# Eight small tiles of the second expert pass, fetched ahead of the weight ring

## The chip, the cores and the metric

The kernel runs on one core of a Trainium2 chip. The metric is device time in microseconds, the median of several runs; less is better.

## The reference

Two encoder layers over 512 frames of 1024 channels. Each has a token mixer (a convolution module in layer 0, a short gated convolution in layer 1) and then a mixture of experts; each part is wrapped in a conditioned residual and a layer norm. The change lies in the experts:

```python
g_idx = argmax(xf @ w_group + b_group)          # one of 4 groups for each frame
e_logits = (xf @ w_router + b_router)           # 32 experts, 8 in each group
top_p, top_e = top_k(softmax(e_logits of the group), 2)
hid = silu(xblk @ w_gate[e]) * (xblk @ w_up[e]) # w_gate, w_up: 1024 x 512
yb = hid @ w_down[e]                            # w_down: 512 x 1024
y = sum over a frame's two experts of weight * yb
```

All is float32, so an expert's three matrices are 6 MB and a layer's 32 experts 192 MB.

## The kernel before

**Passes.** The experts of a layer are handled in 14 passes (`PASSES`). A pass has 128 slots for frames, in four groups of 32 columns, shared by one to four experts: pass 0 has two experts with 64 slots each, pass 1 four experts with 32 each, pass 2 one expert with all 128. Experts are put in order of the number of frames that chose them, except that the first two places always hold experts 0 and 1, so that pass 0 can be fetched before anything is known of the routing. The other places' experts are known when the tile `ids` has been written (L1076); SyncE then loads the numbers of a pass into registers (`experts`, L154 to L160) when it comes to the first fetch of that pass.

**The ring.** All large weights go through the tag `ring` of six buffers of 2 MB (`R`, L107). `todo` lists the fetches in order; `pump` starts fetches while fewer than six units are out, `unit` takes the next one for use, and `done` gives one back and pumps. All these fetches are issued by SyncE, in the order of the list. A unit of an expert pass (`u_pass`, L169) holds two parts of 1 MB. Parts come in the order of `parts_of_pass` (L165): for the first half of the contraction the gate matrices of all the pass's experts, then their up matrices; the same for the second half; then the two halves of the down matrices. Pass 1 so has 24 parts, 0 to 23: 0 to 3 the four experts' first gate halves, and so on. A part's 8 KB for one partition are four rows of a matrix that lie one after another.

**A pass.** The loop over `t` from 0 to 15 (L1252) multiplies the slots with gate and up. Four steps of `t` share the parts of one kind; after the fourth, `release` gives back the ring units that are used up. In between, the loop issues other work for TensorE: `gather` of the next passes' inputs, `combine`, which adds the results of the pass before to the frames, and in pass 1 at `t == 1` the four scaling rows (`row`, L444) with which GpSimd scales the residual. Then come `hid`, its transposes and the down matmuls (L1327), and the results are scaled (L1339) and split into two float32r tiles each (`split`, L455) for `combine` in the next pass.

**Small tiles.** The tag `w2` has 21 buffers of 256 KB, for everything small that is passed between engines (`W`, L76): the logits' copies, one-hot matrices, rows, split results. An allocation takes a buffer that has come free; what first writes it waits for the last reader of what was there.

Before the last pass a branch (`beyond`, L1200) handles experts with more frames than slots; at this branch SyncE waits until its fetches have landed.

Of the kernel before, what the change touches and what calls it, by code (L numbers as in the profile page):

```python
# [37 lines left out]
RING = 6  # L38
NW2 = 21
LAST = 4  # L40
BIG = 1e30
FAR = 4096.0

PASSES = ((2, 2), (1, 1, 1, 1), (4,), (2, 2), (3, 1), (2, 2), (3, 1), (2, 1, 1), (2, 2), (3, 1), (2, 2), (3, 1),
          (2, 2), (1, 1, 1, 1))
# [17 lines left out]
def trunk_kernel(ctx: ExitStack, tc: tile.TileContext, x, c, ada_w, ada_b, a_w_in, a_b_in, a_w_dw, a_b_dw,  # L63
# [3 lines left out]
    nc = tc.nc  # L67
# [5 lines left out]
    def T(shape, dt, tag, bufs=1):  # L73
        return sb.tile(shape, dt, name=tag, tag=tag, bufs=bufs)

    def W(shape, dt=F32):  # L76
        return sb.tile(shape, dt, name="w2", tag="w2", bufs=NW2)
# [6 lines left out]
    def P(tag, shape=(128, 512)):  # L84
        return pp.tile(list(shape), F32, name="p" + tag, tag=tag, bufs=PB[tag])
# [5 lines left out]
    todo, have = deque(), deque()  # L91
# [8 lines left out]
    def unit():  # L100
        return have.popleft()

    def done(n=1):
        state["out"] -= n
        pump()

    def R(shape):  # L107
        return sb.tile(shape, F32, name="ring", tag="ring", bufs=RING)
# [10 lines left out]
    def u_ada1(i, v, kq):  # L119
        def f():  # L120
            t = R([128, 4, D])
            w = ada_w[i, kq * 512:(kq + 1) * 512, v * D:(v + 1) * D].rearrange("(k p) n -> p k n", p=128)
            for z in (slice(0, 3), slice(3, 4)) if kq else (slice(0, 4),):
                nc.sync.dma_start(t[:, z], w[:, z])
            return t
        return f
# [10 lines left out]
    def u_bin(nb):  # L137
        def f():
            t = R([128, 3, KD, 128])
            for z, part in enumerate((1, 2, 0)):  # L140
                nc.sync.dma_start(t[:, z], b_w_in[0, :, part * D + nb * 128:part * D + nb * 128 + 128]
                                  .rearrange("(k p) n -> p k n", p=128))
            return t
        return f

    def u_out(w, h):
        def f():
            t = R([128, 4, D])
            nc.sync.dma_start(t, w[h * 512:(h + 1) * 512, :].rearrange("(k p) n -> p k n", p=128))
            return t  # L150
        return f


    def experts(i, g):  # L154
        if g == 0:
            return [slice(0, 1), slice(1, 2)]
        if (i, g) not in ids:
            ids[i, g] = [bass.ds(nc.values_load(ids[i][:1, p:p + 1], engines=[ET.SP], min_val=0, max_val=NE - 1), 1)
                         for p in range(FIRST[g], FIRST[g] + len(PASSES[g]))]
        return ids[i, g]  # L160
# [4 lines left out]
    def parts_of_pass(n):  # L165
        return [(s, z, h) for h in range(2) for z in range(2) for s in range(n)] + \
               [(s, 2, u) for u in range(2) for s in range(n)]

    def u_pass(i, g, j):  # L169
        def f():  # L170
            t = R([128, 2, 2048])
            for y, (s, z, h) in enumerate(parts_of_pass(len(PASSES[g]))[2 * j:2 * j + 2]):
                w = (e_w_gate, e_w_up, e_w_down)[z][i, experts(i, g)[s]]
                nc.sync.dma_start(t[:, y], w.rearrange("o (p h k) n -> h p (o k n)", h=2, k=2 if z == 2 else 4)[h])  # L174
            return t
        return f


    def u_last(i, d):
        def f():  # L180
            n = len(PASSES[-1])
            t = R([128, n, 2, 512])
            for s, e in enumerate(experts(i, NP - 1)):
                nc.sync.dma_start(t[:, s], e_w_down[i, e].rearrange("o (p h k) n -> h p (o k) n", h=2, k=2)
                                  [1][:, :, d * 512:(d + 1) * 512])
            return t
        return f
# [9 lines left out]
    for i in range(DEPTH):  # L197
        if i == 1:
            todo += [u_bin(nb) for nb in range(2)]
            for nb in range(2, KD):  # L200
                todo += [u_ada1(1, 1 + nb // 2, nb % 2), u_bin(nb)]
        else:
            todo += [rest.popleft()]
        todo += [u_out((a_w_out, b_w_out)[i][0], h) for h in range(2)]
        todo += list(rest) if i == 0 else []
        todo += [u_ada1(1, v, kq) for v in ((1, 0), (5,))[i] for kq in range(2)]
        for g in range(NP):
            n = len(PASSES[g])
            if g < NP - 1:
                todo += [u_pass(i, g, j) for j in range(3 * n)]  # L210
            else:
                todo += [u_pass(i, g, j) for j in range(5 * n // 2)] + [u_last(i, d) for d in range(2)]

# [100 lines left out]
    for kind in set(PASSES):  # L314
        if len(kind) > 1:
            t = side[kind] = T([128, len(kind)], F32, "side%d" % (len(side),))
            V.memset(t, 0.0)
            o = 0
# [113 lines left out]
    def mod(i, v):  # L432
        return mods[i][:, v * 8:v * 8 + 8]
# [82 lines left out]
    class Out:  # L516
# [28 lines left out]
        def run(self, uT, pre, uh, ul, extra, turn, copies, logits, choose, fill, hook):  # L545
# [16 lines left out]

            last = range(KD - LAST, KD)

# [71 lines left out]
    for k in range(KD):  # L636
        p = P("a")
# [104 lines left out]
    w = None  # L742
    for nb in range(KD):
        if nb % 2 == 0:
            w = unit()
        s = slice((nb % 2) * 128, (nb % 2) * 128 + 128)
# [31 lines left out]
        if nb == 2:  # L778
            p = P("c")
# [49 lines left out]
    res = Out(grow, False)  # L829
# [27 lines left out]
    for i in range(DEPTH):  # L857
# [63 lines left out]
        def choose():  # L921
            for _ in zip_longest(first_max(e1, Fl(m1), El, Fl(kk)), first_max(go, gm, Lg, kg)):
                pass
            V.scalar_tensor_tensor(Ew, o1, -BIG, Ew, op0=OP.mult, op1=OP.add)
            for _ in first_max(e2, Fl(m2), El, Fl(kk)):
# [138 lines left out]
        t = by_expert(0)  # L1064
# [156 lines left out]
                PE.matmul(sums[q][d], ident, half(q, d), start=True, stop=False)  # L1221

        pend = None
        for g, kind in enumerate(PASSES):
            Q, j = g // 2, g % 2
            ns = len(kind)
# [2 lines left out]
            cols, o = [], 0  # L1229
# [8 lines left out]


            def piece(y):  # L1240
                while len(tiles) <= y // 2:
                    tiles.append(unit())
                return tiles[y // 2][:, y % 2].rearrange("p (k n) -> p k n", k=4)

            def release(y):
                nonlocal free
                while 2 * free + 2 <= y:
                    done()
                    free += 1

            pgu = [P("a"), P("a")]
            for t in range(2 * KD):  # L1252
                z, k = t // 4 % 2, t // 8 * 4 + t % 4
                if t % 4 == 0:
                    w = [piece(t // 4 * ns + s) for s in range(ns)]
                for s, a, b in cols:
                    PE.matmul(pgu[z][a:b, :], xe(Q, k, j)[:, a:b],  # L1257
                              w[s][:, t % 4, :], start=k == 0,
                              stop=k == KD - 1)
                if t % 4 == 3:  # L1260
                    release((t // 4 + 1) * ns)
                if g == 1:
                    if t == 1:
                        arow, brow = row(pcol("mg", i * 8, 8), ALPHA), row(pcol("mb", i * 8, 8), ALPHA)
                        for q in range(NQ):
                            scale_rows(q, arow, brow)
                    if t in (3, 6):
                        gather(1, 0 if t == 3 else 2)
                    for item in {7: (0,), 9: (1, 2), 11: (3, 4), 13: (5, 6)}.get(t, ()):
                        combine(pend, item)  # L1270
                elif t in (4, 8, 12):
                    combine(pend, t // 2 - 2)
                    combine(pend, t // 2 - 1)
                if g == 0:
                    if t in (1, 4):
                        gather(0, {1: 4, 4: 6}[t])
                    elif t == 6:
                        weigh()
                    elif t == 11:
                        counts()  # L1280
                        ohs.append(pair(1, Vd))
                if i == 0 and g == NP - 1 and t == 1:
                    nxt_aff = affine(pcol("fg", 0, 8), pcol("fb", 0, 8), mod(1, 1), mod(1, 0))
                if i == DEPTH - 1 and g == NP - 1 and t == 13:
                    arow, brow = row(pcol("fg", i * 8, 8)), row(pcol("fb", i * 8, 8))
                if t == 12 and g:
                    ws, C = slots_of(ohq, FIRST[g], kind)
# [15 lines left out]
            if g == 0:  # L1303
                GF = row(mod(i, 5))
                t = by_expert(1)
# [10 lines left out]
            for u in range(2):  # L1316
                last = g == NP - 1 and u == 1
                if last:
                    w = [unit(), unit()]
                    w = [[w[d][:, s] for d in range(2)] for s in range(ns)]  # L1320
                else:
                    w = [piece((4 + u) * ns + s) for s in range(ns)]
                    w = [[v.rearrange("p (f d) n -> p f d n", d=2)[:, :, d] for d in range(2)] for v in w]
                for x in range(4):
                    f, d = (x % 2, x // 2) if last else (x // 2, x % 2)
                    for s, a, b in cols:
                        PE.matmul(pd[d][a:b, :], hT[:, (2 * u + f) * 128 + a:(2 * u + f) * 128 + b], w[s][d][:, f, :],  # L1327
                                  start=u + f == 0, stop=u + f == 2)
# [11 lines left out]
            for d in range(2):  # L1340
                y = W([128, 512], F32R), W([128, 512], F32R)
# [20 lines left out]
        if i == DEPTH - 1:  # L1362
            for n in range(NQ + 1):
# [9 lines left out]
                for h in range(2):  # L1373
                    t = half(q, h)
# [41 lines left out]
        w = unit()  # L1416
# [48 lines left out]
        for nb in range(KD):  # L1465
# [31 lines left out]
            if nb == KD - 1:  # L1497
# [3 lines left out]
                res = Out(grow, True)  # L1501
# [8 lines left out]
            t = W([128, 512])  # L1510
# [35 lines left out]
```

## Time and profile before

| | us |
|---|---|
| median of 3 runs | 1492.92 (1492.81 to 1493.61) |
| profiled execution | 1491.18 |
| its span, first to last instruction | 1489.4 |

The profile is that of one execution. Times in its views are microseconds from the start of the span. PE is TensorE's matmul, PEld its weight load, DVE VectorE, ACT ScalarE, POOL GpSimd, SP SyncE; a "q" behind an engine's name is its sequencer, on which transfers are issued. A line number such as L1257 is a line of the kernel before. A float32 matmul of the program shows as two. A view of windows gives, for stretches of the span, each engine's busy time with the number of its instructions, the clock granted to TensorE, the share of the 16 DMA engines' time that was busy, and the rate.

### The profile page before, as it was taken

The page shows a single profiled execution, that of the slowest core. Times are in us where ns is not written, and L with a number is a line of the kernel's source. Part 1 is how long each engine was busy: PE and PEld are TensorE (multiplying, and loading weights), DVE is VectorE, ACT ScalarE, POOL GpSimd, SP SyncE. Part 2 cuts the span into 40 slices and gives each one's busy share as a digit, 9 for nine tenths or more (in the row PEclk, how much of TensorE's full clock was granted, in tenths as well). Part 3 has the DMA queues.
Part 4 walks back from the last instruction along what each step waited for, and adds up shares of the span by engine and source line. Part 5 has one row for each costly group of instructions (what it writes and reads, how often), then busy time and mean ns, then how long its engine had stood idle before and what let it go on. Part 6 is the DMA issues. An engine that isn't in the chain of part 4 may idle for free. (4 is left out here: it accounts for less than half of the span.)

```text
span 1489.4 us, 20667 instructions
## 1 busy us (share of the span) xinstructions
PE 1382.6 (93%) x8044; PEld 735.5 (49%) x8044; DVE 739.6 (50%) x1426; ACT 325.7 (22%) x547; POOL 263.9 (18%) x275
## 2 busy tenths in 40 slices
PE   4999898999999999997898989999999999999875
PEld 2444477544444444442286767874445444454322
DVE  2799988533343433332267876453334343343215
ACT  1465476210010011000061222422001000011001
POOL 1399942050000000000026051003100000000002
PEclk9999999999999999999999999989999999999988
DMA  8954344799999999999993745239999999999984
GB/s 295 396 213 177 117 154 174 280 420 421 422 419 420 418 421 420 421 421 387 376 279 127 232 173 179 108 147 413 421 421 417 410 416 422 421 421 420 420 356 150
DMA packets 112960, 488.68 MB, mean 328 GB/s; under 512 B 12483, under 2 KB 45771, under 8 KB 63691
## 3 DMA queue, kind: packets, MB, share of 16 engines
q1 hardware_dynamic: 108555, 486.84, 82.1%
q8 instruction: 67, 1.10, 0.3%
q0 software_dynamic: 128, 0.04, 0.2%
q10 hardware_dynamic: 4160, 0.30, 0.2%
q14 instruction: 50, 0.41, 0.1%
HBM read 485.02 MB, written 2.10 MB: 327 GB/s over the span
## 5 line engine op out<-in xcount | busy, mean ns | idle before, releaser
L1257 PE MATMUL pa<-ring,w 128*32 128x512 f32 (+2 forms) x2624 | 438.5, 604 | 26.6 <-DMA ring<-in_e_w_up_dram 15.1
L1131 DVE TENSOR_TENSOR X<-X,pb 128x512 f32<-128x512 f32 x208 | 133.9, 683 | 274.8 <-PE pb L1139 274.8
L1257 PEld LDWEIGHTS pa<-ring,w 128*32 128x32 f32 (+2 forms) x2624 | 120.8, 120 | 274.5 <-issue 227.9
L1327 PE MATMUL pa<-ring,w 128*32 128x512 f32 (+2 forms) x1312 | 209.0, 600 | 9.6 <-DMA ring<-in_e_w_down_dram 6.4
L1139 PE MATMUL pb<-w,w 128*128 128x512 f32 x416 | 130.1, 435 | 0.0
L1327 PEld LDWEIGHTS pa<-ring,w 128*32 128x32 f32 (+2 forms) x1312 | 60.9, 120 | 135.8 <-issue 113.5
L1339 DVE SCALAR_TENSOR_TENSOR w<-pa,ws,w 128x512 f32<-128x512 f32 x56 | 41.9, 750 | 164.9 <-PE pa L1327 162.3
L750 PE MATMUL pa<-RB,ring 128*128 128x512 f32 x256 | 116.5, 612 | 6.2 <-DMA ring<-in_a_w_in_dram 4.2
L1139 PEld LDWEIGHTS pb<-w,w 128*128 128x128 f32 x416 | 72.5, 193 | 97.5 <-issue 80.7
L695 POOL TENSOR_TENSOR w<-w,w 128x512 f32<-128x512 f32 x80 | 104.7, 1309 | 56.2 <-ACT w L693 50.6
L456 ACT ACTIVATE w<-w 128x512 fp32r<-128x512 f32 x58 | 36.6, 630 | 256.8 <-DVE w L1339 256.8
L457 POOL TENSOR_TENSOR RC<-w,RB 128x512 fp32r<-128x512 f32 x8 | 10.9, 1387 | 434.2 <-ACT RB L456 434.2
L1010 ACT ACTIVATE w<-pc,aff 128x256 f32<-128x256 f32 x56 | 31.7, 566 | 253.7 <-PE pc L1005 253.7
L709 DVE SCALAR_TENSOR_TENSOR pb<-RC,w,pb 128x512 f32<-128x512 f32 x126 | 83.6, 745 | 0.0
L750 PEld LDWEIGHTS pa<-RB,ring 128*128 128x128 f32 x256 | 49.1, 196 | 68.8 <-issue 63.3
L1012 DVE TENSOR_SCALAR w<-pc,aff 128x256 f32<-128x256 f32 x56 | 30.5, 544 | 105.8 <-ACT w L1010 105.8
L1289 ACT ACTIVATE w<-pa 128x512 f32<-128x512 f32 x28 | 16.7, 597 | 300.3 <-PE pa L1257 300.3
L1380 POOL TENSOR_TENSOR X<-X,w 128x512 f32<-128x512 f32 x3 | 4.9, 1621 | 426.6 <-ACT X L1379 426.6
L462 PE MATMUL pa<-RB,w 128*128 128x512 f32 x168 | 68.8, 409 | 9.8 <-DVE w L457 9.8
L460 PE MATMUL pa<-RB,w 128*128 128x512 f32 x168 | 68.6, 408 | 0.0
L1005 PE MATMUL pc<-w,RB 128*128 128x256 f32 x448 | 67.1, 295 | 1.5 <-DVE w L977 1.5
L461 PE MATMUL pa<-RC,w 128*128 128x512 f32 x168 | 67.4, 401 | 0.0
(345 smaller groups left out, 1746.1 us busy)
## 6 DMA issues: line engine op xcount, KB each, us to landing
ring<-in_e_w_gate_dram SPq DMA_DIRECT2D x128, 1024.0 KB, 12.6
ring<-in_e_w_up_dram SPq DMA_DIRECT2D x128, 1024.0 KB, 16.1
ring<-in_e_w_down_dram SPq DMA_DIRECT2D x120, 1024.0 KB, 15.8
ring<-in_ada_w_dram SPq DMA_DIRECT2D x14, 2048.0 KB, 11.6
ring<-in_ada_w_dram SPq DMA_DIRECT2D x10, 1536.0 KB, 6.5
ring<-in_b_w_in_dram SPq DMA_DIRECT2D x24, 512.0 KB, 6.5
ring<-in_a_w_in_dram SPq DMA_DIRECT2D x8, 1024.0 KB, 8.2
ring<-in_e_w_down_dram SPq DMA_DIRECT2D x16, 512.0 KB, 13.8
```

What stands on the lines that cost most here:

```text
L460: PE.matmul(p, ah, bh, start=start, stop=False)
L461: PE.matmul(p, ah, bl, start=False, stop=False)
L462: PE.matmul(p, al, bh, start=False, stop=stop)
L695: G.tensor_add(vp, vp, z)
L709: V.scalar_tensor_tensor(t if j == TAPS - 1 else acc[n % 2], a, wj, acc[n % 2], op0=OP.mult, op1=OP.add)
L750: PE.matmul(p, w[:, k, h, s], hT[:, k, :], start=k == 0, stop=k == KD - 1)
L1005: PE.matmul(ps[(k - k0) // 2][:, k % 2], src[:, k, q * 128:(q + 1) * 128], oh(Q, q), start=q == 0 and part == 0 and k % 2 == 0, stop=q == ...
L1131: V.tensor_add(half(q, d), half(q, d), p)
L1139: PE.matmul(p, C[:, q * 128:(q + 1) * 128], ys[d][z], start=z == 0, stop=z == 1)
L1257: PE.matmul(pgu[z][a:b, :], xe(Q, k, j)[:, a:b], w[s][:, t % 4, :], start=k == 0, stop=k == KD - 1)
L1327: PE.matmul(pd[d][a:b, :], hT[:, (2 * u + f) * 128 + a:(2 * u + f) * 128 + b], w[s][d][:, f, :], start=u + f == 0, stop=u + f == 2)
L1339: V.scalar_tensor_tensor(ys[d], pd[d], ws, GF[d], op0=OP.mult, op1=OP.mult)
```

## The change

Two parts of pass 1, 2 MB, are kept in eight tiles of the tag `w2`: for each of the parts 0 and 1 (the first gate halves of the pass's first two experts) four tiles of 128 x 512, one for each of the steps t = 0 to 3. They are fetched in both layers by eight transfers that SyncE issues as soon as the numbers of pass 1's experts can be loaded, ahead of pass 0's loop in program order. The ring's list for pass 1 begins with part 2 and is one unit shorter; `piece` and `release` count accordingly.

```diff
@@ -38,6 +38,7 @@
 RING = 6
 NW2 = 21
 LAST = 4
+FREE = 2
 BIG = 1e30
 FAR = 4096.0
 
@@ -169,11 +170,22 @@
     def u_pass(i, g, j):
         def f():
             t = R([128, 2, 2048])
-            for y, (s, z, h) in enumerate(parts_of_pass(len(PASSES[g]))[2 * j:2 * j + 2]):
+            n = 2 * j + (FREE if g == 1 else 0)
+            for y, (s, z, h) in enumerate(parts_of_pass(len(PASSES[g]))[n:n + 2]):
                 w = (e_w_gate, e_w_up, e_w_down)[z][i, experts(i, g)[s]]
                 nc.sync.dma_start(t[:, y], w.rearrange("o (p h k) n -> h p (o k n)", h=2, k=2 if z == 2 else 4)[h])
             return t
         return f
+
+
+    def small_parts(i):
+        res = []
+        for s, z, h in parts_of_pass(len(PASSES[1]))[:FREE]:
+            w = (e_w_gate, e_w_up, e_w_down)[z][i, experts(i, 1)[s]].rearrange("o (p h k) n -> h p (o k) n", h=2, k=4)[h]
+            res.append([W([128, 512]) for _ in range(4)])
+            for k in range(4):
+                nc.sync.dma_start(res[-1][k], w[:, k, :])
+        return res
 
 
     def u_last(i, d):
@@ -207,7 +219,7 @@
         for g in range(NP):
             n = len(PASSES[g])
             if g < NP - 1:
-                todo += [u_pass(i, g, j) for j in range(3 * n)]
+                todo += [u_pass(i, g, j) for j in range(3 * n - (FREE // 2 if g == 1 else 0))]
             else:
                 todo += [u_pass(i, g, j) for j in range(5 * n // 2)] + [u_last(i, d) for d in range(2)]
 
@@ -1221,6 +1233,7 @@
                 PE.matmul(sums[q][d], ident, half(q, d), start=True, stop=False)
 
         pend = None
+        ahead_parts = small_parts(i)
         for g, kind in enumerate(PASSES):
             Q, j = g // 2, g % 2
             ns = len(kind)
@@ -1238,12 +1251,18 @@
 
 
             def piece(y):
+                if g == 1:
+                    y -= FREE
+                    if y < 0:
+                        return ahead_parts[y + FREE]
                 while len(tiles) <= y // 2:
                     tiles.append(unit())
                 return tiles[y // 2][:, y % 2].rearrange("p (k n) -> p k n", k=4)
 
             def release(y):
                 nonlocal free
+                if g == 1:
+                    y -= FREE
                 while 2 * free + 2 <= y:
                     done()
                     free += 1
@@ -1255,7 +1274,7 @@
                     w = [piece(t // 4 * ns + s) for s in range(ns)]
                 for s, a, b in cols:
                     PE.matmul(pgu[z][a:b, :], xe(Q, k, j)[:, a:b],
-                              w[s][:, t % 4, :], start=k == 0,
+                              w[s][t % 4] if isinstance(w[s], list) else w[s][:, t % 4, :], start=k == 0,
                               stop=k == KD - 1)
                 if t % 4 == 3:
                     release((t // 4 + 1) * ns)
```

## Rows read from the trace of the kernel before

**Rows 1.** The page: span, busy time, and DMA share and GB/s in 40 slices.

```profile
span 1489.4 us, 20667 instructions
...
PE 1382.6 (93%) x8044; PEld 735.5 (49%) x8044; DVE 739.6 (50%) x1426; ACT 325.7 (22%) x547; POOL 263.9 (18%) x275
...
DMA  8954344799999999999993745239999999999984
GB/s 295 396 213 177 117 154 174 280 420 421 422 419 420 418 421 420 421 421 387 376 279 127 232 173 179 108 147 413 421 421 417 410 416 422 421 421 420 420 356 150
```

**Rows 2.** Windows of layer 0: PE, PEld, DVE, ACT, POOL, clock, DMA share, GB/s.

```profile
274.40:282.60 8.20, 8.20 (x49) 4.60 (x48) 1.63 (x3) 1.69 (x3) 0.00 (x0) 1.00 0.00 0
282.70:706.50 423.80, 410.93 (x2562) 185.82 (x2561) 156.82 (x349) 44.81 (x75) 20.20 (x16) 0.99 1.01 417
```

**Rows 3.** The same windows of layer 1.

```profile
992.10:1001.50 9.40, 9.40 (x54) 5.80 (x53) 1.63 (x3) 1.69 (x3) 0.00 (x0) 0.92 0.00 0
1001.60:1427.40 425.80, 410.35 (x2562) 185.62 (x2561) 156.34 (x346) 44.87 (x75) 20.30 (x16) 1.00 1.00 415
```

**Rows 4.** Timeline of SyncE's issues for pass 1: start, us, instruction.

```profile
281.67 0.91 SPq L174 DMA_DIRECT2D ring<-in_e_w_gate_dram  x2
...
287.35 0.85 SPq L174 DMA_DIRECT2D ring<-in_e_w_gate_dram  x2
...
319.71 1.95 SPq L174 DMA_DIRECT2D ring<-in_e_w_down_dram  x4
...
1038.58 1.97 SPq L174 DMA_DIRECT2D ring<-in_e_w_down_dram  x4
```

**Rows 5.** The experts' numbers: timeline of VectorE, and SyncE's loads by line.

```profile
272.59 0.17 DVE L1076 CAST ids<-pa 1x32 int32<-1x32 f32 x1
...
990.51 0.17 DVE L1076 CAST ids<-pa 1x32 int32<-1x32 f32 x1
...
L158 SPq TENSOR_LOAD <-ids x60: 261/267/472, 272.8 to 1379.2; - x60
L158 SPq FUSED_REGOPS  x60: 147/152/183, 273.3 to 1379.5; - x60
```

**Rows 6.** Timeline of TensorE in pass 1, layer 0, then layer 1's last.

```profile
305.01 1.92 PE L1257 MATMUL pa<-ring,w 128*32 128x512 f32 x16
...
336.78 5.53 PE L1327 MATMUL pa<-ring,w 128*32 128x512 f32 x36
...
346.22 3.62 PE L1327 MATMUL pa<-ring,w 128*32 128x512 f32 x26 [1.44 <-DMA ring<-in_e_w_down_dram]
...
1064.82 5.32 PE L1327 MATMUL pa<-ring,w 128*32 128x512 f32 x26 [1.45 <-DMA ring<-in_e_w_down_dram]
```

**Rows 7.** Waits of TensorE for the weights, 350 to 690: total, times, longest.

```profile
PE pa L1257 <- DMA ring<-in_e_w_up_dram: 0.9, 1, 0.9
```

**Rows 8.** The chain that ended last: start, us, what.

```profile
1430.77 10.82 DMA ring<-in_e_w_up_dram
```

**Rows 9.** Windows, columns as in rows 2; the last holds down tiles alone.

```profile
286.00:288.00 2.00, 2.00 (x12) 0.57 (x8) 1.11 (x8) 1.97 (x4) 0.00 (x0) 1.00 0.99 418
288.00:290.00 2.00, 2.00 (x12) 0.72 (x10) 1.86 (x7) 0.12 (x1) 0.00 (x0) 1.00 0.96 287
...
1453.00:1456.00 3.00, 1.86 (x14) 0.84 (x16) 1.83 (x3) 0.00 (x0) 0.00 (x0) 1.00 1.05 387
```

**Rows 10.** Timeline: the logits' last matmuls, and the scaling rows in pass 1.

```profile
255.90 3.72 PE L896 MATMUL pa<-w,w 128*128 128x108 f32 x32
...
308.16 1.07 ACT L451 ACTIVATE w<-pb 128x512 f32<-128x512 f32 x2
...
308.80 1.14 PE L449 MATMUL pb<-ident,colP 128*128 128x128 f32 x8 [0.84 <-ACT w L451]
```

**Rows 11.** A window of layer 1 after the wait, columns as in rows 2.

```profile
1066.00:1067.00 1.00, 1.00 (x8) 0.22 (x4) 0.00 (x0) 0.00 (x0) 0.00 (x0) 0.50 1.02 426
```

**Rows 12.** DMA issues by line: count, KB each, us to landing.

```profile
out_dram<-X SPq DMA_DIRECT2D x8, 256.0 KB, 2.0
```

## The prediction

> **What bounds the kernel now.** I read the page first: TensorE is busy 93% of the span, and the line of GB/s has two long plateaus near 420, one for each layer's experts, with poor stretches between them [rows 1]. The reader should ask at each edge of a plateau who made the weights late.
>
> Windows cut at the edges answer that. In layer 0 the weight stream stands still from 274.4 to 282.6 us, then runs at 417 GB/s and share 1.01 to 706.5 without a hole; in layer 1 it stands from 992.1 to 1001.5 and then runs at 415 GB/s to 1427.4 [rows 2, 3]. So each layer has one dead time of 8 to 9.5 us just before its plateau. Its cause: the ring of six 2 MB tiles is full of the first pass's weights, and the second pass's can't be fetched until a first-pass matmul frees a tile. SyncE issues the first of them at 281.67, though the experts' numbers were written at 272.59 [rows 4, 5]. In layer 1 the numbers come at 990.51 [rows 5] and the stream moves at 1001.6.
>
> The third view is TensorE through the second pass. It goes through both projections without waiting for data until its last down-projection group: it reaches the down matmuls at 336.78, and stands until 346.22, when the last of the pass's 24 pieces of 1 MB has landed; the rest takes 3.6 us and the third pass starts at about 349.8 [rows 6]. Layer 1 does the same, with the last piece at 1064.82. So the third pass starts when the stream has delivered 24 MB after its dead time. From 350 to 690 TensorE waits for that stream for 0.9 us in all [rows 7]: there it runs at its own pace, and the ring, refilled as it frees tiles, keeps the queue from going dry. At the end the last fetch is on the chain that ended last, 1430.77 to 1441.6 [rows 8]. An advance of the 24th piece therefore moves the third pass, the releases that follow it, the rest of the stream and the end by as much, once per layer.
>
> **The change, part by part.** *The early fetch.* Two of the 24 pieces go into eight 256 KB tiles, without a ring tile being needed. Their order on SyncE is: four number loads, eight issues, then the old wait for the ring. The loads are no new work (before makes them at 272.8 too); at 0.27 + 0.15 us plus gaps [rows 5] I take 0.6 us each, so the issues start near 275.3. Two issues take 0.91 us [rows 4], so eight take some 4.5 us, until 279.8. A first packet follows an issue by 1.0 us (281.67 to 282.7) [rows 2, 4]: data from 276.3. Each small transfer writes 2 KB runs into a partition instead of 8 KB; the last down tiles have such runs and moved at 387 GB/s [rows 9], which gives 5.4 us for the 2.10 MB, or 281.7 as the end. That lies inside the dead time, with 1 us to spare; in layer 1 (993.1 + 1.0 + 5.4 = 999.5) with 2 us. So it is costed at nothing. If that cover were gone, each us past 282.7 would delay the ring's stream by a us.
>
> *What it gives.* The ring's stream starts at 282.7 as before but owes two pieces less: 2.10 MB at 417 GB/s are 5.0 us per layer.
>
> *What the ring gives back.* The early tiles are used once. After step t=3 of the second pass the kernel before frees two ring tiles, the new one only one (the other half of what was read sat in small tiles). From there on as many bytes have been asked for as before, while 5.0 us more have been delivered, so the queue is 5.0 us shorter. The critical place is t=7, whose release lets SyncE issue the pieces 16 to 19 at 319.71 (layer 1: 1038.58) [rows 4]. TensorE gets there at its own pace, so this issue doesn't move. Piece 15 landed 8 pieces before the last: 346.2 - 8 x 2.5 = 326.2; with the head start at 321.2, its last packet some tenths before. The new packets start at 319.71 + 1.0 = 320.7: just in time. In layer 1 it is 1064.8 - 20.0 - 5.0 = 1039.8 against 1039.6, the same. What a just-in-time issue costs can be read at 287.35, where the queue of before was about to run dry [rows 4]: the two us from 288 moved 287 GB/s against 418 ahead of them [rows 9], a loss of 2 x (1 - 287/418) = 0.6 us. Bounds: 0 if the queue holds, 1.4 if the whole round of issue and packet (1.0) is exposed and 0.4 of hand-over with it. I take 0.6 in layer 0 and 0.8 in layer 1, where a few tenths less are left.
>
> *The buffers.* The eight tiles come out of the 21 of the tag w2 and are held from the first pass to t=3 of the second. The longest free are those of the logits' copies, whose last reader ended at 255.90 + 3.72 = 259.6 in layer 0 [rows 10], so SyncE doesn't wait for them. Counting what lives at once, I come to 20 of 21, when the split tiles of the first pass's result and the four scaling rows are wanted. These then take buffers that steps t=0 and t=1 have just freed: those matmuls end at 306.9 [rows 6], and the rows are written from 308.16 [rows 10]. Cover: 1.2 us. Gone, ScalarE would stand on that write, behind it the other rows, and TensorE's next transposes, which are already waiting 0.8 us there [rows 10]. I put 0.2 us per layer for this and for eight semaphores where there were two; bounds 0 and 1.2.
>
> *Code.* A list instead of a tile in the matmul's operand: the same number of matmuls, nothing.
>
> **Sum.** Layer 0: 5.0 - 0.6 - 0.2 = 4.2; layer 1: 5.0 - 0.8 - 0.2 = 4.0; together 8.2 us. TensorE allows it: without data waits the third pass could start at 336.78 + 2 x 3.6 = 344.0, 5.8 us earlier. One more term is set to zero: in layer 1 the wait was followed by about 3 us at a granted clock of 0.50 [rows 11], so that the rest took 5.3 us instead of 3.6 [rows 6]. A shorter wait may save these 1.7 us, but only for TensorE; the stream, which decides at the end, isn't moved by it.
>
> The profiled execution took 1491.18 us (span 1489.4 and 1.8 around it), 1.7 below the runs' median of 1492.92. On its own time the forecast is 1483.0; on the median, **1484.7 us**.
>
> **The rivals.**
>
> *All of the head start arrives* (chance 0.15): no dip at t=7 and no buffer wait, and perhaps the clock term: 10.0 to 11.7 us less, 1481.2 to 1482.9. For it: the queue holds by tenths. Against it: the dip at 288.
>
> *Given back* (0.08): the second pass is later at t=7, because ScalarE's splits and rows wait for buffers and the transposes of TensorE behind them. Each us there is lost from the gain, so a delay of 4.2 us per layer makes it 1492.9. Against it: freed at 306.9, wanted at 308.2.
>
> *Slower* (0.04): the small transfers don't overlap. A lone 256 KB store took 2.0 us from issue to landing [rows 12]; eight in a row would end at 276.3 + 16.0 = 292.3, 9.6 us into the ring's stream; less 4.2 gained that is 5.4 late, in layer 1 994.1 + 16.0 - 1001.6 = 8.5, less 4.0, 4.5 late: 1502.8. It decides from (282.7 - 276.3 + 4.2) / 8 = 1.3 us each on. Against it: transfers of 512 KB moved at 387 GB/s [rows 9], that is 1.35 us each, so their fixed times overlapped.
> The Trainium skill speaks for this rival: "DMA: Bandwidth & Descriptors", section Bandwidth, asks for transfers of at least 1 MiB, and its Anatomy section fits 2.0 us plus the bytes at 436 GB/s to one transfer, 2.6 us here. Taken one after another that would be an estimate of 20.8 us and a slower kernel; the trace shows no eight of this size in a row, but its 512 KB rows contradict a fixed time that adds up.
>
> *Only one layer gains, or a bigger dip* (0.15): 3 to 6 us less, 1487 to 1490.
>
> The forecast itself has 0.58, with its own range 1483 to 1486.5. Leaving out 1502.8 and 1492.9 and the rest of the tails, the range for 8 in 10 is 1481.8 to 1489.0. About 0.2% (3.0 us) can be told from no change here: faster 0.87, same 0.09, slower 0.04.
>
> **What would show it.** Right: packets in both dead times beginning some 2 to 3.5 us after the numbers; the ring's stream starting at 282.7 and 1001.6 as before; SyncE's issue of pieces 16 to 19 unmoved at about 319.7; a dip of the GB/s at 321 and 1040; TensorE's last wait in the second pass ending near 342 (before 346.22) and 1060.6; the rest of the plateau without holes, ending near 702 in layer 0. Wrong: small transfers that run past 282.7; a later t=7; holes after 350 where the shorter queue runs dry; or an unmoved end although the second pass ended earlier, which would mean that TensorE's own pace or the last pass sets the time.

## The result, and the profile after

The changed kernel takes 1482.42 us (median of four runs, 1481.76 to 1484.14); the ratio to the kernel before is 0.9947, 95% interval [0.9928, 0.9965], that is 7.9 us less [5.2, 10.7]. The medians themselves lie 10.4 us apart (before, with one run more: 1492.87). The forecast was 1484.7 us and 8.2 us less. The profiled execution took 1484.14 us, span 1482.4, which is 7.0 us less than the profiled execution of before.

The page after; of the GB/s line, one number for each fortieth of the span, mainly the poor stretches moved [rows 1].

```profile
span 1482.4 us, 20744 instructions
...
DMA  8964344899999999999994655349999999999984
GB/s 292 396 227 171 118 155 173 316 400 421 421 419 420 419 420 420 421 420 396 364 273 143 218 193 175 114 167 400 405 421 420 419 418 421 422 420 420 420 364 162
```

SyncE's issues in the kernel after, timeline of both layers (cut at the marks).

```profile
274.51 4.41 SPq L187 DMA_DIRECT2D w<-in_e_w_gate_dram  x8
282.04 0.87 SPq L176 DMA_DIRECT2D ring<-in_e_w_gate_dram  x2
...
320.12 2.40 SPq L176 DMA_DIRECT2D ring<-in_e_w_down_dram  x4
...
992.16 4.37 SPq L187 DMA_DIRECT2D w<-in_e_w_gate_dram  x8
...
1037.56 2.12 SPq L176 DMA_DIRECT2D ring<-in_e_w_down_dram  x4
```

For the eight small ones of layer 0 (L187) the view by tile gives the spread of the issues and the time to landing; the trace holds the landings of the last three only.

```profile
L187 SPq DMA_DIRECT2D w<-in_e_w_gate_dram x8: 332/333/368, 274.5 to 278.6; - x8
...
DMA to landing us min/median/max: 5.8/5.9/6.0
```

Windows of their transfer in layer 0, columns as in [rows 2]:

```profile
276.00:278.00 2.00, 2.00 (x11) 0.52 (x9) 0.61 (x2) 0.56 (x1) 0.00 (x0) 1.00 0.89 313
278.00:280.00 2.00, 2.00 (x18) 1.92 (x16) 0.00 (x0) 0.00 (x0) 0.00 (x0) 1.00 0.70 197
280.00:282.00 2.00, 2.00 (x12) 0.77 (x12) 0.54 (x1) 0.56 (x1) 0.00 (x0) 1.00 0.85 262
```

The eight issues stand where SyncE used to wait for the ring, and the ring's own issues have not moved by more than TensorE has (282.04 against 281.67, 320.12 against 319.71 [rows 4]; pass 0 began 0.37 us later in this execution).

To see how far ahead the stream is, cut windows that begin 2 us ahead of the first matmul of pass 0 (275.73 and 994.66 us before, 276.10 and 993.55 after): 42 us, and the 10 us behind them, in which the t=7 release falls (the ring units given back after step t=7 of pass 1). Columns as in [rows 2]; the last is GB/s. First the kernel before, both layers.

```profile
273.73:315.73 42.00, 40.96 (x258) 20.71 (x260) 13.71 (x43) 11.18 (x19) 6.57 (x6) 1.00 0.79 316
315.73:325.73 10.00, 10.00 (x73) 4.46 (x66) 2.52 (x4) 1.03 (x2) 9.77 (x8) 1.00 1.01 424
...
992.66:1034.66 42.00, 40.95 (x254) 20.70 (x257) 13.69 (x43) 11.24 (x19) 6.68 (x6) 0.99 0.79 317
1034.66:1044.66 10.00, 10.00 (x73) 4.51 (x66) 2.52 (x4) 1.02 (x2) 9.75 (x8) 1.00 1.02 424
```

The same windows of the kernel after.

```profile
274.10:316.10 42.00, 40.91 (x252) 20.69 (x255) 13.70 (x43) 11.17 (x19) 6.85 (x7) 0.98 0.93 364
316.10:326.10 10.00, 10.00 (x77) 4.42 (x66) 2.52 (x4) 0.99 (x2) 9.76 (x8) 1.00 0.86 337
...
991.55:1033.55 42.00, 40.91 (x254) 20.70 (x257) 13.72 (x43) 11.17 (x19) 6.85 (x7) 0.99 0.94 368
1033.55:1043.55 10.00, 10.00 (x77) 4.42 (x66) 2.52 (x4) 0.99 (x2) 9.77 (x8) 1.00 0.82 315
```

The first window says that the head start came whole: 364 - 316 = 48 GB/s over 42 us are 2.0 MB in layer 0, and 368 - 317 give 2.1 MB in layer 1; at 420 GB/s that is 4.8 and 5.1 us. The second says that much of it was lost again: 424 - 337 over 10 us are 0.87 MB or 2.1 us, 424 - 315 are 1.09 MB or 2.6 us. What is left is 2.7 and 2.5 us.

The hole in single microseconds of layer 0, after:

```profile
318.00:319.00 1.00, 1.00 (x10) 0.88 (x8) 0.00 (x0) 0.00 (x0) 0.92 (x2) 1.00 0.96 401
319.00:320.00 1.00, 1.00 (x9) 0.16 (x8) 0.27 (x1) 0.56 (x1) 1.00 (x2) 1.00 0.51 213
320.00:321.00 1.00, 1.00 (x10) 0.45 (x10) 0.41 (x2) 0.00 (x0) 0.94 (x1) 1.00 0.20 82
321.00:322.00 1.00, 1.00 (x13) 0.26 (x8) 0.55 (x1) 0.00 (x0) 0.98 (x1) 1.00 1.02 213
322.00:323.00 1.00, 1.00 (x10) 0.42 (x3) 0.00 (x0) 0.00 (x0) 1.00 (x2) 1.00 0.89 344
323.00:324.00 1.00, 1.00 (x8) 0.41 (x10) 0.63 (x2) 0.00 (x0) 0.92 (x2) 1.00 1.01 426
```

The rate falls from 319 on, a microsecond before the issue at 320.12, though the last transfer on order (issued at 312.79, 9.41 us to landing) lands only at 322.20; and after the issue it takes until 323 to be whole again. The queue was not full until its last byte and then empty: it thinned out at the end and built up at the start.

Before, TensorE had two waits for down pieces at the end of pass 1; the first of the two, both layers, timeline (the second is in [rows 6]):

```profile
343.74 1.05 PE L1327 MATMUL pa<-ring,w 128*32 128x512 f32 x2 [1.43 <-DMA ring<-in_e_w_down_dram]
...
1062.32 1.05 PE L1327 MATMUL pa<-ring,w 128*32 128x512 f32 x2 [1.44 <-DMA ring<-in_e_w_down_dram]
```

After, one is left. It and the start of pass 2, timeline, both layers.

```profile
343.54 3.62 PE L1346 MATMUL pa<-ring,w 128*32 128x512 f32 x26 [1.44 <-DMA ring<-in_e_w_down_dram]
347.09 3.27 PE L1276 MATMUL pa<-ring,w 128*128 128x512 f32 x7
...
1061.21 3.62 PE L1346 MATMUL pa<-ring,w 128*32 128x512 f32 x26 [1.44 <-DMA ring<-in_e_w_down_dram]
1064.76 3.70 PE L1276 MATMUL pa<-ring,w 128*128 128x512 f32 x8
```

Counted from the start of pass 0 the wait ends at 343.54 - 276.10 = 67.44 us where it was 346.22 - 275.73 = 70.49, and in layer 1 at 67.66 where it was 70.16 [rows 6]: 3.05 and 2.50 us, what the bytes say. Layer 1 has a second gain: the rest of the pass takes 3.62 us again instead of 5.32 [rows 6], because the clock stays at 1.00 (2.4 GHz) where it had fallen to 0.50, 1.2 GHz [rows 11]. From the start of pass 0 to that of pass 2 (here called the stretch), that makes 74.04 - 70.99 = 3.05 and 75.41 - 71.21 = 4.20 us, 7.25 together, against 7.04 of the whole execution. That they agree so closely is partly luck: outside its two stretches an execution takes from 1338.2 to 1340.7 us in the fourteen profiles of this document.

### The profile page after: what moved, and what is told of

It reads as the page before. It is cut to its first block, busy times and chain, and to the rows that moved or that the text cites. A ratio compares the mean times of both kernels' runs of the same rounds, so it can differ in the third digit from the quotient of the medians.

```text
span 1482.4 us, 20744 instructions
## 1 busy us (share of the span) xinstructions
PE 1376.9 (93%) x8044; PEld 733.1 (49%) x8044; DVE 740.2 (50%) x1426; ACT 325.5 (22%) x547; POOL 264.4 (18%) x275
```

## The experiments

The first theory: the gain is the dead time put to use, less the hole at t=7, and the clock adds to it where the waits of before had brought it down. Rivals: one layer or the clock makes it all; the tiles, not the time of the fetch, make it; the stream is not limited at t=7. All twelve kernels below were timed in turn with the kernel before; ratios are to it, with 95% intervals. The stretch is that of each kernel's profiled execution, layer 0 / layer 1; an asterisk marks a clock of 0.50 at its end. "Gathers moved" is also called the reordered change.

| kernel | us, median | ratio | stretch, us |
|---|---|---|---|
| before (first profile) | 1492.87 | 1 | 74.04 / 75.41* |
| after (first profile) | 1482.42 | 0.9947 [0.9928, 0.9965] | 70.99 / 71.21 |
| after again | 1484.23 | 0.9949 [0.9930, 0.9968] | 71.00 / 71.13 |
| early fetch in layer 0 only | 1487.54 | 0.9974 [0.9963, 0.9985] | 71.26 / 75.51* |
| in layer 1 only | 1487.45 | 0.9966 [0.9954, 0.9977] | 75.51* / 71.06 |
| same tiles, fetched late | 1491.63 | 1.0002 [0.9990, 1.0015] | 74.03 / 75.40* |
| after, gathers moved | 1480.71 | 0.9927 [0.9906, 0.9947] | 69.03 / 68.69 |
| before, gathers moved | 1490.11 | 0.9989 [0.9974, 1.0004] | 75.80* / 75.30* |
| after, t=7 delayed | 1487.23 | 0.9976 [0.9963, 0.9989] | 73.47 / 73.44 |
| before, t=7 delayed | 1490.39 | 0.9991 [0.9979, 1.0003] | 75.36 / 73.71 |
| one part only | 1490.69 | 0.9992 [0.9977, 1.0007] | 74.92* / 73.48 |
| one part, gathers moved | 1482.53 | 0.9935 [0.9919, 0.9951] | 71.71 / 71.07 |
| gathers moved, numbers read in turn | 1481.83 | 0.9927 [0.9911, 0.9943] | 69.83 / 69.22 |
| gathers moved, again | 1480.58 | 0.9922 [0.9906, 0.9938] | 71.51 / 69.43 |

**One layer at a time, and the change again.** `FREE` becomes a pair, (2, 0) or (0, 2), read as `FREE[i]`:

```diff
-FREE = 2
+FREE = (2, 0)
...
-            n = 2 * j + (FREE if g == 1 else 0)
+            n = 2 * j + (FREE[i] if g == 1 else 0)
```

> Early fetch of the eight small tiles in layer 0 only. If the gain of each layer comes from its own dead time (what both traces show: 1.82 MB are there by 282.7 us, 4.35 us of the stream at 417 GB/s, of which the dip at 310 to 330 us takes back 2.0), pass 2 of layer 0 starts some 2.7 us earlier than before and layer 1 runs as in the kernel before: 2 to 3 us less in all, ratio 0.9980 to 0.9987. If the whole gain of 7.9 us is that of layer 1 or of the clock there, this run shows no gain (0.9995 to 1.0005). If layer 0 carries it all, 0.995.

> Early fetch in layer 1 only. By the first theory its last wait of pass 1 ends some 2.6 us earlier and the clock stays at full speed over the start of pass 2, which gives another 1.7 us: 3.5 to 4.5 us less, ratio 0.9970 to 0.9977, and the gains of this run and of the one with layer 0 alone add up to that of the whole change within its interval. If the clock has no part in it, 2.6 us (0.9983) and pass 2 starts at half clock as in the kernel before.

> The changed kernel once more, as the measure for the other three on the same chip: 0.9947 if its first timing holds (0.9930 to 0.9965).

Each layer gains by itself: 0.26% and 0.34%, together 0.60%, against 0.51% for both at once, within the intervals. Both are somewhat above what was expected, by less than their intervals. The stretches are as clean: 71.0 to 71.3 us in every layer with the early fetch, 74.0 or 75.4 to 75.5 in every one without (first five rows of the table). That the gain was one layer's or only the clock's is out.

In the run with layer 1 alone it is layer 0 whose clock falls, which it had not done in the profile of before. Its timeline of TensorE:

```profile
344.18 1.04 PE L1346 MATMUL pa<-ring,w 128*32 128x512 f32 x2 [1.45 <-DMA ring<-in_e_w_down_dram]
346.66 5.32 PE L1346 MATMUL pa<-ring,w 128*32 128x512 f32 x26 [1.44 <-DMA ring<-in_e_w_down_dram]
```

And a window behind the wait, the clock third from the end:

```profile
347.00:349.00 2.00, 2.00 (x12) 0.42 (x8) 0.00 (x0) 0.00 (x0) 0.00 (x0) 0.50 1.03 430
```

Two waits for two pieces one after the other, and then half the clock. Over all the profiles, layers with both waits lost the clock in 7 of 11 cases and those with one such wait or none in 0 of 17. The two waits shrink to one with the early fetch, so the change also removes a risk, worth 5.32 - 3.62 = 1.7 us a time. Over many executions 7 of 11 would make some 1.1 us a layer (an estimate from these counts), and with the 2.7 and 2.5 us of the bytes 7.4 us for the change, near the 7.6 to 7.9 that the ratios give. The Trainium skill ("TensorE: Matmul & The Clock Gate", section HAM oscillation — how this bites in real kernels) describes the same pattern, waits for DMA that throw the engine to its lower clock just before the next burst; the rows here agree, though the wait that it describes is a single and longer one, and here it was two of 1.4 us.

**The same tiles, fetched late.**

```diff
-        ahead_parts = small_parts(i)
+        ahead_parts = None
...
                     release((t // 4 + 1) * ns)
+                if g == 0 and t == 3:
+                    ahead_parts = small_parts(i)
```

> The same eight tiles, transfers and matmul operands in both layers, but the eight transfers are issued only behind the first ring unit that pass 0 releases, so that the queue stays dead from the experts' numbers to that release. If the head start is the whole of the gain and small transfers and tiles cost next to nothing, this is as fast as the kernel before: 0 to 0.5 us more, ratio 0.9997 to 1.0005, with no dip at the t=7 release. If the gain is from the tiles themselves (two parts more in flight), a gain of over 2 us stays. If small transfers cost, this run is slower by 2 us or more.

Nothing gained and nothing lost, as the first theory has it. Its windows of layer 0, cut as above, are those of the kernel before, without a hole:

```profile
276.04:318.04 42.00, 40.91 (x258) 20.69 (x260) 13.70 (x43) 11.16 (x19) 6.86 (x7) 1.00 0.79 314
318.04:328.04 10.00, 10.00 (x77) 4.43 (x66) 2.52 (x4) 1.00 (x2) 9.77 (x8) 1.00 1.01 421
```

So the eight tiles, the 256 KB transfers and the list in the operand cost nothing that can be measured here; the time of the fetch is all of it.

**The t=7 release earlier.** In pass 1 the two gathers for pass 2, 2.1 us each, go behind the release:

```diff
-                    if t in (3, 6):
-                        gather(1, 0 if t == 3 else 2)
+                    if t in (8, 10):
+                        gather(1, 0 if t == 8 else 2)
```

> The changed kernel with the two gathers of the second pass put behind its steps t=8 and t=10 instead of t=3 and t=6, so that the ring's release at t=7 comes about 4.2 us earlier (two gathers of 2.1 us). If the queue running low before that release costs the 2.0 and 2.4 us that the bytes of both layers show, the hole closes and the stream is 2 us ahead; of that the last wait of pass 1 (1.4 us) can give back 1.4 us in each layer: from the start of pass 0 to that of pass 2 69.6 us instead of 71.0 to 71.2, 2.8 us less in all than the changed kernel, ratio 0.992 to 0.994 to the kernel before. If the dip is not what bounds it, 71.0 and 0.995 as the changed kernel.

> The kernel before with the same move of the two gathers. By the first theory its queue holds 5 us of transfers at that release, so that an earlier release brings nothing: 74.0 to 75.5 us from pass 0 to pass 2, 0 +- 0.7 us in all (0.9995 to 1.0005). If the order of the gathers is better in itself, this run gains the 2 to 3 us too (0.998).

The changed kernel with the gathers moved, layer 0, cut as above:

```profile
274.66:316.66 42.00, 40.92 (x250) 19.39 (x249) 13.15 (x42) 10.60 (x18) 6.87 (x7) 0.98 0.93 364
316.66:326.66 10.00, 10.00 (x72) 5.76 (x72) 3.06 (x5) 1.59 (x3) 9.77 (x8) 1.00 1.02 427
```

The hole is closed: 427 GB/s where it was 337, with the head start as before. The time is 0.9927, and the kernel before gets nothing that can be measured from the same move (0.9989, the interval holds 1). So the hole at t=7 is shown, and it is the shorter queue that makes it. With the hole closed TensorE has no wait for the down pieces left in this execution: its stretch of 69.03 us is 5.0 shorter than that of before.

**The t=7 release later.** 16 gather matmuls more at t=5 of pass 1, whose result nobody reads:

```diff
+                    if t == 5:
+                        extra = P("c", (128, 2, 256))
+                        for _ in range(1):
+                            for part, src in enumerate((nh, nl)):
+                                for k in range(2):
+                                    for q in range(NQ):
+                                        PE.matmul(extra[:, k], src[:, k, q * 128:(q + 1) * 128], oh(1, q),
...
```

> The changed kernel with one more set of 16 gather matmuls, whose result is not used, ahead of the t=6 step of the second pass: it holds up the t=7 release by 2.1 us. By the first theory the stream waits for that release already, so that the whole delay goes into the stream: 2.1 us more in each layer from pass 0 to pass 2 (73.1 to 73.3), 4 us in all, ratio 0.9975. By the rival, that the stream doesn't wait there, the last wait of 1.4 us swallows most of it: 0.7 us a layer, 0.996.

> The kernel before with the same 16 matmuls. Its queue has 5 us in hand at the t=7 release and its two waits of 1.4 us swallow 2.1 us of TensorE's work: nothing lost, 74.0 us from pass 0 to pass 2; in a layer where the two waits brought the clock down to 0.5 the shorter idle time can even keep it up and give back 1.4 us (74.0 instead of 75.4). In all 0 to 2 us less: ratio 0.9985 to 1.0005. If the queue has no such margin, 2 to 4 us more (1.002).

Windows of layer 0, the changed kernel with the delay, then the kernel before with it:

```profile
275.46:317.46 42.00, 40.92 (x255) 20.48 (x253) 13.70 (x43) 11.17 (x19) 6.85 (x7) 1.00 0.92 364
317.46:327.46 10.00, 10.00 (x78) 5.74 (x78) 1.73 (x3) 0.56 (x1) 9.77 (x8) 1.00 0.65 241
```

```profile
273.92:315.92 42.00, 40.97 (x255) 20.51 (x253) 13.69 (x43) 11.16 (x19) 6.58 (x6) 1.00 0.79 316
315.92:325.92 10.00, 10.00 (x74) 5.69 (x78) 1.77 (x3) 0.56 (x1) 9.77 (x8) 1.00 1.00 417
```

Counted from the start of pass 0, the release's first issue comes at 46.24 us where it came at 44.02. In the changed kernel the hole grows from 0.87 to (424 - 241) x 10 = 1.83 MB, by 2.3 us for 2.2 us of delay, and 4 of the 7.6 us gained are gone. The kernel before loses 0.07 MB and nothing in time that can be measured. The early fetch has spent the queue's reserve: the same disturbance costs nothing measurable before and its full length after. One size was off: layer 0 of the delayed kernel before shows a stretch of 75.36 us at full clock, 1.3 more than expected. By the count of bytes its stream was only 0.2 us late; its last piece landed when more bytes of later pieces had come in (26.6 MB from 2 us ahead of pass 0 to the end of the last wait, where the first profiles of before and after have 26.1 and 26.0). Why is open.

**Half of it.** One part of 1 MB, four tiles, instead of two; the last half unit of the ring is released with the pass.

```diff
-FREE = 2
+FREE = 1
...
-            todo += [u_pass(i, g, j) for j in range(3 * n - (FREE // 2 if g == 1 else 0))]
+            todo += [u_pass(i, g, j) for j in range(3 * n - 0)]
...
-                while 2 * free + 2 <= y:
+                while 2 * free + 2 <= y + (g == 1 and y == 6 * ns - FREE):
```

> Only the first of the two parts is held in small tiles (1.05 MB, four tiles, four transfers a layer). The ring goes by pairs of parts, so that up to the t=7 release of the second pass one part fewer is on order than in the kernel before, and the stream is ahead by 1.05 MB (2.5 us). The traces so far: from the t=7 issue to the landing of the last transfer then on order it was 6.6 us in the kernel before (no dip), 4.1 us with its t=7 release delayed (0.2 us lost), 2.1 us in the changed kernel (2.0 us lost). Here it would be 6.6 - 2.5 - 2.5 = 1.6 us, some 2.5 us lost, and so nothing gained: 73.5 to 74.5 us from the start of pass 0 to that of pass 2, ratio 0.9990 to 1.0005. By the rival, gain in proportion to the bytes fetched early, 72.5 us and 0.9975.

> The same single part, with the two gathers behind t=8 and t=10 so that the t=7 release comes 4.2 us earlier. 5.8 us would be on order at the release, no dip, and the 2.5 us of the early part stay: 71.5 us from pass 0 to pass 2, ratio 0.996 to 0.997, between the kernel before and the reordered change (69.0). If the second part is of no use once the gathers are moved, 69.0 and 0.993.

Layer 0 of the single part, then of the single part with the gathers moved:

```profile
275.60:317.60 42.00, 40.87 (x258) 20.69 (x260) 13.73 (x43) 11.18 (x19) 6.88 (x7) 1.00 0.86 341
317.60:327.60 10.00, 10.00 (x75) 4.44 (x66) 2.52 (x4) 0.99 (x2) 9.76 (x8) 1.00 0.85 329
```

```profile
274.58:316.58 42.00, 40.87 (x256) 19.39 (x254) 13.21 (x42) 10.62 (x18) 6.87 (x7) 1.00 0.86 340
316.58:326.58 10.00, 10.00 (x72) 5.75 (x72) 3.06 (x5) 1.56 (x3) 9.77 (x8) 1.00 1.01 424
```

Half the bytes don't bring half the gain. 341 - 316 are 1.05 MB more, and 424 - 329 are 0.95 MB lost in the hole: nothing is left, as worked out from the transfers on order, and 0.9992 is no change. With the gathers moved the megabyte stays and the run comes to 0.9935. That is some 4 us better than its expectation. About 1.8 of them are the clock, which the expectation had forgotten: layer 1 kept it, 75.41 - 71.07 = 4.3 us instead of 2.5. The rest stays open: the two stretches are 2.3 + 4.3 = 6.7 us shorter, the ratio says 9.7.

**The reordered change, the numbers read in turn.** SyncE reads one expert's number, issues its four transfers, then the next, and the other two numbers last; the gathers are moved as above. The second kernel is the reordered change again.

```diff
+        for s, z, h in parts_of_pass(len(PASSES[1]))[:FREE]:
+            load(FIRST[1] + s)
+            w = (e_w_gate, e_w_up, e_w_down)[z][i, known[s]].rearrange(
...
+        for s in range(FREE, len(PASSES[1])):
+            load(FIRST[1] + s)
```

> The changed kernel with the two gathers moved, and SP reads one expert's number, issues its four transfers, reads the next, and reads the last two numbers behind the eight transfers: the first transfer is issued 1.7 us earlier (three reads of 0.58 us). With the gathers moved no wait of TensorE for weights is left in the first two passes, so that TensorE's own work bounds them: nothing more, 69 us from pass 0 to pass 2, ratio to the reordered change 1.000 (0.9927 to the kernel before). If the weights are still what is late, 1 to 1.7 us a layer, 0.991.

> The changed kernel with the two gathers moved once more, as the measure for the other three: 0.9927 (0.9906 to 0.9947) and 68.7 to 69.0 us from pass 0 to pass 2.

No difference, 0.9927 and 0.9922. The reason is simpler than the expected one. Layer 0 of the first, SyncE's timeline:

```profile
273.50 5.09 SPq L192 DMA_DIRECT2D w<-in_e_w_gate_dram  x8
282.77 0.87 SPq L176 DMA_DIRECT2D ring<-in_e_w_gate_dram  x2
```

And one window of it, with 23 GB/s:

```profile
282.00:283.00 1.00, 1.00 (x8) 0.29 (x4) 0.04 (x1) 0.00 (x0) 0.00 (x0) 1.00 0.06 23
```

The 2 MB were there by 282 and the stream then stood still until the ring's first packet. Fetched in either order they are 2 MB, and their being complete earlier is of no use. More would need more bytes, so more buffers; that was not tried.

The reordered change is the best version: 1480.6 to 1480.7 us, 0.9922 to 0.9927, about 0.2% below the change as made (0.9947 and 0.9949). The two were not timed against each other directly, and their intervals overlap a little; that the hole is closed rests on the windows. Its two executions differ by 2.5 us in layer 0's stretch (69.03 and 71.51), though by bytes the stream of the second was only 0.6 us behind (360 and 420 GB/s in the same windows, 0.24 MB less): there the last piece landed when more bytes of later pieces had come in (26.9 MB, counted as above), as in the delayed kernel before. The Trainium skill ("DMA: Bandwidth & Descriptors", section Why a DMA increments its semaphore by 16 and not by 1) says that a transfer runs on up to 16 DMA engines that finish independently, and has landed only when all of them have reported. That would fit; no view here shows the 16 apart.

## Why the prediction came out

- **The bound.** Right: the third pass waits for the stream, and the dead time ahead of it is what the early fetch fills. The late fetch and the single layers show it. One reading was loose: TensorE doesn't stand from 336.78 to 346.22, it works there with two waits, 2.9 us by the profile; and the most that the stretch gave, with no such wait left, was 5.0 us, not the 5.8 that I allowed.
- **The head start, 5.0 us.** Right in size, 4.8 and 5.1. Its timing was off: the last small transfer landed at 278.6 + 6.0 = 284.6, not 281.7. The term that was mis-sized is the 387 GB/s: the eight moved at 197 to 313, some 240 over the 8.7 us from their first packet to their last, while the ring's 1 MB pieces of before, 3.3 us after their first packet at 282.7, moved at 418 [rows 9]. Why the small ones are slower here is open. I had called transfers past 282.7 a sign of being wrong, each us a us lost; they weren't, since 2.0 of the 2.1 MB were ahead all the same: the last small ones and the ring's first were under way together.
- **The hole at t=7, 0.6 and 0.8 us.** The place, the time and the cause were right, the size was not: 2.1 and 2.6 us, outside even the bound of 1.4. The step that failed is "The new packets start at 319.71 + 1.0 = 320.7: just in time". It took a queue to be full until its last landing and whole again with its first packet. The rows show it thin from 319 and whole from 323. In terms of what was still on order at the issue, counted from the issue to the landing of the last earlier transfer, the runs give: 6.6 us (before), nothing lost; 5.6 and 6.0 (gathers moved), nothing; 4.1 (delayed before), 0.2 us; 1.0 to 2.9 (five layers with the change as made; 2.1 in the one above), 2.0 to 2.6 us.
- **Buffers, 0.2 us.** Less: TensorE's wait at the scaling rows went from 0.84 [rows 10] to 0.89 us, and the late fetch cost nothing.
- **The clock, 0.** Wrong: 1.7 us in layer 1. I set it to zero because "the stream, which decides at the end, isn't moved by it". But from pass 2 on TensorE decides: from the start of pass 2 to that of pass 13 it took 335.7 to 337.4 us in both layers of all fourteen profiles, however early the stream was. My own reading of [rows 7] said so; after, TensorE's waits for weights there are 1.3 us. So what the stretch gains reaches the end, from data or from the clock: from profile to profile the two stretches together go from 137.7 to 151.1 us, the rest of the execution only from 1338.2 to 1340.7.
- **The sum.** 4.2 + 4.0 was forecast; the parts measure 4.8 - 2.1 and 5.1 - 2.6 + 1.7, 2.7 and 4.2. Two errors, 3.3 us of hole and 1.7 of clock, were of opposite sign, and the total landed closer than its terms deserve; that is luck. By the medians of the first timing, 10.4 us, it even lies just outside the forecast's own range, among the times of "All of the head start arrives"; timed again the medians are 6.9 us apart (1491.13 and 1484.23). The time alone could not have told the rivals apart; the windows do.
- **The rivals.** "All of the head start arrives" became true only with the gathers moved. Of "Only one layer gains, or a bigger dip" the second half is what happened: with the hole as measured and no clock the sum would have been 2.7 + 2.5 = 5.2 us, within its 3 to 6. "Given back" did not happen. "Slower", that the small transfers don't overlap, is out: of the eight of 256 KB, issued 0.6 us apart, the last three took 5.8 to 6.0 us each and landed 0.6 us apart. The advice of the Trainium skill that it leaned on ("DMA: Bandwidth & Descriptors", section Bandwidth), transfers of at least 1 MiB, cost no time to ignore here (late fetch: 1.0002), though the rate of some 240 GB/s goes its way. The fit of 2.0 us and 436 GB/s, which I took from the Anatomy section of that page of the Trainium skill, is given there for transfers issued by GpSimd, and these are SyncE's.

## What to carry to other kernels

Dead time in a weight stream can be filled with buffers that are idle for other reasons, but a stream that is further ahead has a shorter queue: find the next release that it now depends on and move work behind it, or the gain leaks out there. Price a queue that runs short by its thin end and its slow start, not by the time to the first packet. And where TensorE sets its own pace downstream, count what a shorter wait does to its clock.

## What was not expected of the hardware

The queue needed some 4 us of transfers on order at the moment of the next issue to keep its rate (4.1 us: 0.2 us lost; 1.0 to 2.9 us: 2.0 to 2.6 us lost), and a release delayed by 2.2 us then cost 2.3 us. After the refill at 320.12 the stream took about 3 us to reach its full rate: 82, 213 and 344 GB/s in the microseconds from 320 on, then 426. Eight transfers of 256 KB alone on the queue moved at some 240 GB/s. The clock fell in 7 of 11 cases after two waits of 1.4 us with a microsecond of matmuls between them, and in none of 17 with one such wait or none.
